# Token rows on SP's queue, the overflow loop moved from the end to expert pair 10, and a new order of scatter and turning in a one-core mixer + MoE kernel

## The chip, the cores and the metric

One core of a Trainium2 chip runs the whole kernel. The metric is device time in microseconds (us) of one execution. The engines are TensorE (PE, with PEld for its weight loads), VectorE (DVE), ScalarE (ACT), GpSimd (POOL) and SyncE (SP, which only issues DMAs here); a "q" behind a name is that engine's sequencer or DMA queue. All arithmetic is float32, with float32 split in two where the program calls for more exactness.

## The reference, cut to what matters

512 tokens of width 1024, one layer. A hybrid mixer of four branches comes first; then a two-level mixture of experts, which the change touches: 4 groups of 8 experts, each token takes the best group and in it the best two experts.

```python
x = x + g1 * hybrid_mixer(rms_norm(x) * (1 + sc1) + sh1, ...)
h = rms_norm(x) * (1 + sc2) + sh2
g_p, g_idx = top_k(softmax(h @ wg + bg), 1)
top_v, top_i = top_k(expert logits of that group, 2)
gate = g_p * softmax(top_v)
for each expert e, on its tokens xe:                 # 32 experts, D = 1024, inner width 512
    y = (silu(xe @ w1[e]) * (xe @ w3[e])) @ w2[e]
    x += g2 * (gate * y summed back onto the tokens)
```

## The kernel before

**Mixer and routing.** Up to about 790 us the mixer runs; its weights come on SP's queue. The last output projection (`w_out`) and the router's logits are computed in two halves of 256 tokens. `route(half)` (L1132) finds groups, experts, gates and ranks of a half on DVE; for each of its two 128-token tiles ACT writes the normalised rows into the one buffer `xg[0]` (L1145) and stores them to the DRAM table `xhd` (L1147, ACT's queue in before). Route of half 1 runs under a hand-written order of DVE; `meanwhile()` (L1111) puts a few matmuls without a user (`scr`) on PE between the two steps of that route, as many as `WARM` says. `toki` holds, for each pair of experts, the 128 token numbers (64 for each expert); `fetch(p)` (L1122) gathers these rows from `xhd` into `xg[p % 2]`, on POOL's queue.

**Expert stream.** The experts are taken two at a time, as 16 pairs p. A pair's weights are 12 tiles of 1 MB in the order of use: 8 for `front` (w1, w3), 4 for `product` (w2); pair 15 has 18, most of them smaller, so that there are 198 loads in all. They land in a ring of 20 SBUF slots. `stream()` (L1089) hands tile i out and calls `load_to(i + 20)` (L1080), so the load of tile i + 20 is issued on SP (L1086) as soon as its slot is free. The compiled program counts these loads on eight counters in turn (DMAHW0 to DMAHW7): load n goes out when load n-8 has landed.

**Loop over pairs** (L1489 on), PE's order written out by hand: `product(p-1)` (two groups of matmuls into `py`), `parts(p-1)` (DVE and ACT split `py` into `yh` and `yl`), `front(p)` (64 matmuls into `ph`), then `add` of pair p-1: for each half of the columns and each of 4 token tiles t two matmuls into `po` (PE) that scatter the rows back by the 0/1 matrix `pT`, and one DVE addition into `xm` (L1408). Among the adds stand `turn_in(p+1)` (L1327: eight PE transposes of `xg` into `xT`, eight evacuations into `xe`, odd ones on DVE and even ones on ACT, then `fetch(p+2)`) and `turn` (L1370: four transposes of `g`, evacuated into `gT`).

**Overflow.** 64 slots for each expert hold the usual load. Tokens past that are handled by `overflow()` (L1413): a loop on the chip (`For_i`, L1418) whose count `n_ob` is read at run time from `eobi`. In before it stands behind pair 15's front and adds and ahead of pair 15's four products. With these inputs the count is zero: the trace has not one `ov` weight load of the loop's body.

Of the kernel before, what the change touches and what calls it, by code (L numbers as in the profile page):

```python
# [9 lines left out]
F32 = mybir.dt.float32  # L10
F32R = mybir.dt.float32r
# [11 lines left out]
KD = D // 128  # L23
NT = S // 128
# [5 lines left out]
RL = (10, 11, 18, 19)  # L30
WS = (10, 3, 6, 6, 12)
LATE = 4
WARM = (1, 2, 2, 2, 4)
LNEXP = "natural_log_exp_and_others"


# [1 line left out]
def trunk(ctx, tc, x, c, ada_w, ada_b, norm1_g, norm2_g, w_in, hgrn_lb, hgrn_norm_g, conv_w, conv_b, conv_ln_g,  # L38
          conv_ln_b, sb_qnorm_g, sb_knorm_g, ret_norm_g, w_branch, w_gate, b_gate, w_out, router_group_w,
          router_group_b, router_expert_w, router_expert_b, expert_w1, expert_w3, expert_w2, out):  # L40
    nc = tc.nc
# [169 lines left out]
    for t in range(NT):  # L211
        A.activation(sq0, xt[t], AF.Square, accum_out=ssq[:, t:t + 1])
    pe_order = ctx.enter_context(ExitStack())
# [3 lines left out]
        engines={mybir.EngineType.DVE, mybir.EngineType.Activation}))  # L217
# [814 lines left out]
    xhd = dram.tile([S, D], F32, name="xhd")  # L1032
# [17 lines left out]
    ewx = ctx.enter_context(tc.tile_pool(name="ewx", bufs=EWX, side="right"))  # L1050
# [24 lines left out]
    ring = [(ewx, "ew")] * EWX + [(wst, tag) for tag in ("raw", "raw", "wh", "wh", "wl", "wl")]  # L1075
# [4 lines left out]
    def load_to(n):  # L1080
        while len(loaded) < min(n, len(order)):
            pool, tag = ring[len(loaded) % len(ring)]
            w = pool.tile([128, 2048], F32, name="ew", tag=tag)
            src = order[len(loaded)]
            w = w[:, :src.shape[1] * src.shape[2]].rearrange("p (k c) -> p k c", k=src.shape[1])
            nc.sync.dma_start(w, src)  # L1086
            loaded.append(w)
# [34 lines left out]
    def fetch(p):  # L1122

        P.indirect_dma_start(out=xg[p % 2], out_offset=None, in_=xhd[:, :],  # L1124
                             in_offset=bass.IndirectOffsetOnAxis(ap=toki[:, p:p + 1], axis=0),
                             bounds_check=S - 1, oob_is_err=False)
# [5 lines left out]
    def route(half, pl, between=None):  # L1132
# [10 lines left out]
        for i in range(2):  # L1143
            xs = xg[0]
            A.activation(xs, xm[:, 2 * half + i], AF.Copy, scale=r[:, i:i + 1])  # L1145
            t = 2 * half + i
            nc.scalar.dma_start(xhd[t * 128:(t + 1) * 128], xs)  # L1147
        gm, gi, og = first_max(lg[:, :, :4], 4, "f0")
        then(og[:, 1])
        ge = nr.tile([128, 2, 4], F32, name="ge", bufs=2)  # L1150
# [19 lines left out]
        for i in range(2):  # L1170
            t = 2 * half + i
# [77 lines left out]
    pe_order = ctx.enter_context(ExitStack())  # L1249
    for half in range(2):  # L1250
        pl = ps_o.tile([128, 512], F32, name="pl", tag="o1")
        ts = slice(2 * half, 2 * half + 2)
        cbs = (0, 1, 2, 3) if half == 0 else (2, 3, 0, 1)
        for n, cb in enumerate(cbs):
            if half == 0 or cb < 2:
                wo[cb] = wblock(w_out, 0, KD, cb * 256, 256)
            w = wo[cb]
            if half and n == 3:
                load_to(EWX)
            cs = slice(cb * 256, cb * 256 + 256)  # L1260
            o = psm()
            for i in range(2):
                three(o[:, i * 256:(i + 1) * 256],
                      tuple((lambda k, a=a: a[:, k, i * 128:(i + 1) * 128]) for a in (mh[half], ml[half])),
                      tuple((lambda k, a=a: a[:, k, :]) for a in w), KD, first=i == 0)
            y = yo[n % 2]
            V.tensor_mul(y, o.rearrange("p (t c) -> p t c", t=2), g1b[:, None, cs].to_broadcast([128, 2, 256]))
            (V if half else P).tensor_add(xm[:, ts, cs], xm[:, ts, cs], y)
            for i in range(2):
                A.activation(y[:, i], xm[:, 2 * half + i, cs], AF.Square,  # L1270
                             accum_out=sq2[:, 2 * half + i, cb:cb + 1])
            if n:
                logits(half, pl, n - 1, cbs[n - 1])
        between = None
        if half:
            pe_order.enter_context(tc.manual_schedule(engines={mybir.EngineType.PE}))
            between = meanwhile()
        logits(half, pl, 3, cbs[3], between)
        if half:
            next(between)  # L1280
        if half:
            with tc.manual_schedule(engines={mybir.EngineType.DVE}):
                route(half, pl, between.send)
        else:
            route(half, pl)

# [38 lines left out]
    ew = stream()  # L1325

    def turn_in(p):  # L1327

        pt = psz("xT").rearrange("p a (b c) -> p (a b) c", c=128)
        xe = moe.tile([128, KD, 128], F32, name="xe", bufs=1)  # L1330
        for d in range(KD):
            a, k = divmod(d, 4)
            T.transpose(pt[:, d], xg[p % 2][:, a * 512 + k:(a + 1) * 512:4], ident)  # L1333
        for d in range(KD):
            if d % 2:
                V.tensor_scalar(xe[:, d], pt[:, d], a2s[:, d:d + 1], sh2s[:, d:d + 1], op0=OP.mult, op1=OP.add)
            else:
                A.activation(xe[:, d], pt[:, d], AF.Identity, scale=a2s[:, d:d + 1], bias=sh2s[:, d:d + 1])
        if p < 14:
            fetch(p + 2)  # L1340
        return xe

    def front(p, xe):

# [14 lines left out]
    class Back:  # L1359
# [10 lines left out]
        def turn(self):  # L1370
            pg = ps_o.tile([128, 512], F32, name="gTp", tag="o1")
            for f in range(4):
                T.transpose(pg[:, f * 128:(f + 1) * 128], self.g[:, f::4], ident)
            self.gT = moe.tile([128, 512], F32, name="gT", tag="yh") if self.p < 15 else ewx.tile([128, 512], F32, name="gT", tag="ew")
            A.activation(self.gT, pg, AF.Copy)

        def product(self, n):
# [35 lines left out]
    def overflow():  # L1413
# [2 lines left out]
        base = keep.tile([128, 1], F32, name="base")  # L1416
        V.memset(base, 0.0)
        with tc.For_i(0, n_ob) as i:  # L1418
            e = nc.sync.value_load(eobi[0:1, bass.ds(i, 1)], min_val=0, max_val=31)

            def wload(src, kk, c0):
                w = moe.tile([128, 512], F32, name="ov", tag="yl")
                r0 = kk // 4 * 512
                nc.sync.dma_start(w, src[0][bass.ds(e, 1), r0:r0 + 512, c0:c0 + 512].rearrange(
                    "o (p k) c -> p k (o c)", k=4)[:, kk % 4])
                return w

            sk = keep.tile([128, 2, NT], F32, name="s4", bufs=2)
            V.tensor_scalar(sk, oslot, base, None, op0=OP.subtract)
            pr_ = moe.tile([128, NT, 128], F16, name="pr_", tag="pT", bufs=1)  # L1430
            e0_ = moe.tile([128, 512], F32, name="e0_", tag="yh")
            gt_ = moe.tile([128, NT, 128], F32, name="gt_", tag="yh")
            for t in range(NT):
                V.tensor_scalar(e0_[:, :128], io[:, :128], sk[:, 0, t:t + 1], None, op0=OP.is_equal)
                V.scalar_tensor_tensor(pr_[:, t], io[:, :128], sk[:, 1, t:t + 1], e0_[:, :128], op0=OP.is_equal,
# [12 lines left out]
            V.tensor_scalar(toki[:, 0:1], pg_[:, 2:3], 1024.0, None, op0=OP.add)  # L1448
            fetch(0)
            V.tensor_scalar(go[:, 1:2], pg_[:, 2:3], 1024.0, None, op0=OP.add)  # L1450
            pT = ewx.tile([128, 512], F32R, name="ovpT", tag="ew")
            V.tensor_scalar(pT, io, go[:, 1:2], None, op0=OP.is_equal)
            xo = moe.tile([128, KD, 128], F32, name="xe", bufs=1)
            ps = psz("ovx")
# [5 lines left out]
            for j, src in enumerate((expert_w1, expert_w3)):  # L1460
                for kk in range(KD):
                    mm(ph[:, j], xo[:, kk], wload(src, kk, 0), kk == 0, kk == KD - 1)
            g = moe.tile([128, 512], F32, name="g", tag="yh")
            A.activation(g, ph[:, 0], AF.Sigmoid)
            V.tensor_mul(g, g, ph[:, 0])
            V.scalar_tensor_tensor(g, g, go[:, 0:1], ph[:, 1], op0=OP.mult, op1=OP.mult)
            pg = psm("ovT")
            for f in range(4):
                T.transpose(pg[:, f * 128:(f + 1) * 128], g[:, f::4], ident)
            gT = moe.tile([128, 512], F32, name="gT", tag="yh")  # L1470
            A.activation(gT, pg, AF.Copy)
            for hf in range(2):
                cs = slice(hf * 512, hf * 512 + 512)
                py = psm("ovy")
                for kk in range(4):
                    mm(py, gT[:, kk * 128:(kk + 1) * 128], wload(expert_w2, kk, hf * 512), kk == 0, kk == 3)
                V.tensor_mul(py, py, g2b[:, cs])
                yh = moe.tile([128, 512], F32R, name="yh", tag="yh")
                yl = moe.tile([128, 512], F32R, name="yl", tag="yl")
                split(yh, yl, py)  # L1480
                for t in range(NT):
                    po = psm("ovo")
                    mm(po, pT[:, t * 128:(t + 1) * 128], yh, True, False)
                    mm(po, pT[:, t * 128:(t + 1) * 128], yl, False, True)
                    V.tensor_add(xm[:, t, cs], xm[:, t, cs], po)
            V.tensor_scalar(base, base, 128.0, None, op0=OP.add)


    b, nxt = None, turn_in(0)  # L1489
    for p in range(16):  # L1490
        if b:
            for n in range(2):
                b.product(n)
            for n in range(2):
                b.parts(n)
            b.places()
        xe = nxt
        g = front(p, xe)
        if p == 1:
            eobi, oslot = overflow_tables()  # L1500
        late_, b = b, Back(p, g)
        if late_:
            late_.add(0, (0, 1, 2))
        if p < 15:
            nxt = turn_in(p + 1)
        if late_:
            late_.add(0, (3,))
            late_.add(1, (0,))
        b.turn()
        if late_:  # L1510
            late_.add(1, (1, 2, 3))
    pe_order.close()
    overflow()
    pe_order.enter_context(tc.manual_schedule(engines={mybir.EngineType.PE}))
    b.places()
    for n in range(4):
        b.product(n)
# [27 lines left out]
```

## Time and profile before

| | us |
|---|---|
| median of 3 runs | 1298.15 (1297.8 to 1303.95) |
| the profiled execution, its own time | 1301.55 |
| span of that execution, first to last instruction | 1299.8 |
| PE busy in the span | 1230.8 (95%) |
| DVE busy | 692.3 (53%) |
| ACT busy | 467.0 (36%) |
| POOL busy | 210.7 (16%) |

The expert stream fills the stretch from about 827 to 1275 us. The mean shares hide that PE and the DMA engines are both near their limit there, so rows are read by stretch, and idle time is read with the wait that ended it: `[4.74 <-SPq L1418]` behind a row means that the engine stood 4.74 us before it and that an event of SP's sequencer at line 1418 released it.

### The profile page before, as it was taken

To read this page: it belongs to the slowest core of one execution; us is meant where nothing else is said; L and a number is where in the kernel's file an instruction comes from. 1 tells how busy PE (TensorE), PEld (TensorE's weight loads), DVE (VectorE), ACT (ScalarE), POOL (GpSimd) and SP (SyncE) were. 2 spreads that over 40 slices of the span, in tenths; PEclk is the share of its full clock that TensorE was granted. 3 is DMA by queue.
4 is the path that set the end of the run, shared out by engine and by line. 5 is a ranking of instruction groups with operands and counts; after the bars stand their busy time and mean duration, and the time that the engine had idled before them with its cause. 6 is when DMAs were issued, how large, how long until landed. Compare 5 with 4: busy or idle time off the path is not lost. (4 is left out here: it accounts for less than half of the span.)

```text
span 1299.8 us, 17074 instructions
## 1 busy us (share of the span) xinstructions
PE 1230.8 (95%) x6818; PEld 855.0 (66%) x6818; DVE 692.3 (53%) x1105; ACT 467.0 (36%) x665; POOL 210.7 (16%) x171
## 2 busy tenths in 40 slices
PE   7999988999999999998999999799999999999997
PEld 5789888987779987787888897333333433333344
DVE  2724679998963564457865435235333443433334
ACT  3447565446544455453335533111111111111110
POOL 3226746201110111212211110100000000000000
PEclk8999997999999999999999999899999999999998
DMA  9332311132222322226775298699999999999994
GB/s 337 130 120 66 97 40 59 33 97 66 77 86 66 98 65 73 89 90 211 234 232 185 92 386 342 246 416 419 420 418 419 420 419 419 419 419 419 420 403 161
DMA packets 108477, 299.23 MB, mean 230 GB/s; under 512 B 9704, under 2 KB 65112, under 8 KB 84588
## 3 DMA queue, kind: packets, MB, share of 16 engines
q1 hardware_dynamic: 102312, 289.45, 58.5%
q10 hardware_dynamic: 3300, 4.36, 1.0%
q0 software_dynamic: 2784, 4.31, 1.0%
q8 instruction: 54, 0.88, 0.3%
q14 instruction: 27, 0.22, 0.0%
HBM read 298.08 MB, written 4.20 MB: 233 GB/s over the span
## 5 line engine op out<-in xcount | busy, mean ns | idle before, releaser
L58 PE MATMUL ph<-ew,xe 128*64 128x512 f32 x1024 | 229.8, 597 | 7.2 <-DMA ew<-in_expert_w_dram 6.6
L58 PEld LDWEIGHTS ph<-ew,xe 128*64 128x64 f32 x1024 | 77.4, 138 | 156.6 <-issue 135.3
L58 PE MATMUL mm<-hh,wh 128*128 128x512 f32 x448 | 178.8, 399 | 0.0
L254 DVE TENSOR_TENSOR wl<-raw,wh 128x2048 fp32r<-128x2048 f32 x55 | 131.8, 2396 | 85.6 <-ACT wh L253 83.9
L58 PE MATMUL mm<-hh,wl 128*128 128x512 f32 x448 | 174.9, 390 | 1.6 <-DVE wl L266 1.6
L58 PE MATMUL mm<-hl,wh 128*128 128x512 f32 x448 | 174.8, 390 | 0.0
L1408 DVE TENSOR_TENSOR xm<-xm,po 128x512 f32<-128x512 f32 (+1 forms) x136 | 85.8, 648 | 153.5 <-PE po L58 153.3
L253 ACT ACTIVATE wh<-raw 128x2048 fp32r<-128x2048 f32 x55 | 105.2, 1912 | 70.4 <-PE mm L58 70.0
L58 PE MATMUL mm<-wh,hh 128*128 128x256 f32 x448 | 130.4, 291 | 0.0
L58 PE MATMUL mm<-wl,hh 128*128 128x256 f32 x448 | 127.4, 284 | 0.0
L58 PE MATMUL mm<-wh,hl 128*128 128x256 f32 x448 | 127.4, 284 | 0.0
L58 PE MATMUL py<-ew,gT 128*64 128x512 f32 (+1 forms) x544 | 117.6, 586 | 5.4 <-SPq L1418 4.7
L58 PEld LDWEIGHTS mm<-hh,wh 128*128 128x128 f32 x448 | 84.2, 188 | 23.5 <-issue 7.2
L58 PEld LDWEIGHTS mm<-hh,wl 128*128 128x128 f32 x448 | 84.1, 188 | 19.7 <-DVE wl L266 1.9
L58 PEld LDWEIGHTS mm<-hl,wh 128*128 128x128 f32 x448 | 84.2, 188 | 16.5 <-DVE hl L206 0.3
L58 PEld LDWEIGHTS mm<-wh,hh 128*128 128x128 f32 x448 | 86.5, 193 | 6.0 <-issue 5.8
L58 PEld LDWEIGHTS py<-ew,gT 128*64 128x64 f32 x544 | 38.8, 142 | 75.7 <-issue 72.7
L58 PEld LDWEIGHTS mm<-wl,hh 128*128 128x128 f32 x448 | 86.6, 193 | 0.2
L58 PEld LDWEIGHTS mm<-wh,hl 128*128 128x128 f32 x448 | 86.5, 193 | 0.0
L1124 POOL DMA_INDIRECT xg<-xhd,toki x16 | 16.0, 1000 | 394.6 <-PE xT L1333 346.5
L157 ACT ACTIVATE yh<-py 128x512 fp32r<-128x512 f32 (+1 forms) x34 | 19.5, 572 | 160.1 <-DVE py L1396 160.1
L1354 ACT ACTIVATE g<-ph 128x512 f32<-128x512 f32 x16 | 9.6, 598 | 176.3 <-PE ph L58 176.3
(435 smaller groups left out, 2055.8 us busy)
## 6 DMA issues: line engine op xcount, KB each, us to landing
ew<-in_expert_w_dram SPq DMA_DIRECT2D x186, 1024.0 KB, 19.9
raw<-in_w_in_dram SPq DMA_DIRECT2D x26, 1024.0 KB, 4.9
raw<-in_w_gate_dram SPq DMA_DIRECT2D x16, 1024.0 KB, 5.6
adaw<-in_ada_w_dram SPq DMA_DIRECT2D x64, 256.0 KB, 3.4
aw<-in_ada_w_dram SPq DMA_DIRECT2D x32, 256.0 KB, 5.4
raw<-in_w_branch_dram SPq DMA_DIRECT2D x8, 1024.0 KB, 5.7
raw<-in_w_out_dram SPq DMA_DIRECT2D x6, 1024.0 KB, 6.0
ew<-in_expert_w_dram SPq DMA_DIRECT2D x12, 512.0 KB, 12.9
```

Of the source, the lines that this page charges most:

```text
L58: T.matmul(o, l, r, start=start, stop=stop, skip_group_check=True)
L157: A.activation(h_ap, src, AF.Copy)
L253: a = A.activation(wh, raw, AF.Copy)
L254: v = V.tensor_sub(wl, raw, wh.bitcast(F32))
L1124: P.indirect_dma_start(out=xg[p % 2], out_offset=None, in_=xhd[:, :], in_offset=bass.IndirectOffsetOnAxis(ap=toki[:, p:p + 1], axis=0), bo ...
L1354: A.activation(g, ph[:, 0], AF.Sigmoid)
L1408: V.tensor_add(xm[:, t, cs], xm[:, t, cs], po)
```

## The change

1. `WARM[3]` goes from 2 to 0: two of the matmuls without a user go.
2. The four stores of token rows to `xhd` move from ACT's queue to SP's (L1147), and SP joins DVE in the hand-written order around route of half 1, with `load_to(len(ring))` inside it. So the first weight loads are issued on SP among and behind the stores.
3. `turn_in` becomes a generator in two steps: transposes and `fetch(p+2)`; later the evacuations into `xe`, now all on ACT (for pair 0 still on both).
4. The loop over pairs places all four `add(0)` ahead of the transposes of `turn_in`, and the evacuations behind `turn`.
5. `overflow()` moves behind pair 10's front and adds (`OVP = 10`). For pair 11 the transposes, `fetch(12)` and the evacuations stand behind it. The loop's reads and weight loads go to POOL's queue, and its tiles take other buffers; the `gT` of pair 15 uses the common buffer `yh`.

```diff
-WARM = (1, 2, 2, 2, 4)
+WARM = (1, 2, 2, 0, 4)
+OVP = 10
...
-            nc.scalar.dma_start(xhd[t * 128:(t + 1) * 128], xs)
+            nc.sync.dma_start(xhd[t * 128:(t + 1) * 128], xs)
...
-            with tc.manual_schedule(engines={mybir.EngineType.DVE}):
+            with tc.manual_schedule(engines={mybir.EngineType.DVE, mybir.EngineType.SP}):
                 route(half, pl, between.send)
+                load_to(len(ring))
...
     def turn_in(p):
...
             T.transpose(pt[:, d], xg[p % 2][:, a * 512 + k:(a + 1) * 512:4], ident)
+        if p < 14 and p != OVP:
+            fetch(p + 2)
+        yield
+        xe = moe.tile([128, KD, 128], F32, name="xe", bufs=1)
         for d in range(KD):
-            if d % 2:
+            if d % 2 and not p:
                 V.tensor_scalar(xe[:, d], pt[:, d], ...)
             else:
                 A.activation(xe[:, d], pt[:, d], AF.Identity, ...)
-        if p < 14:
-            fetch(p + 2)
-        return xe
+        yield xe
...
-            self.gT = moe.tile([128, 512], F32, name="gT", tag="yh") if self.p < 15 else ewx.tile([128, 512], F32, name="gT", tag="ew")
+            self.gT = moe.tile([128, 512], F32, name="gT", tag="yh")
...
-            e = nc.sync.value_load(eobi[0:1, bass.ds(i, 1)], min_val=0, max_val=31)
+            e = nc.gpsimd.value_load(eobi[0:1, bass.ds(i, 1)], min_val=0, max_val=31)
...
-        xe = nxt
         g = front(p, xe)
         if p == 1:
             eobi, oslot = overflow_tables()
+        nxt = turn_in(p + 1) if p < 15 else iter(())
         late_, b = b, Back(p, g)
         if late_:
-            late_.add(0, (0, 1, 2))
-        if p < 15:
-            nxt = turn_in(p + 1)
+            late_.add(0)
+        if p != OVP:
+            next(nxt, None)
         if late_:
-            late_.add(0, (3,))
             late_.add(1, (0,))
         b.turn()
+        if p != OVP:
+            xe = next(nxt, None)
         if late_:
             late_.add(1, (1, 2, 3))
-    pe_order.close()
-    overflow()
-    pe_order.enter_context(tc.manual_schedule(engines={mybir.EngineType.PE}))
+        if p == OVP:
+            pe_order.close()
+            overflow()
+            fetch(p + 2)
+            pe_order.enter_context(tc.manual_schedule(engines={mybir.EngineType.PE}))
+            next(nxt)
+            xe = next(nxt)
```

In the rows of the order, `L1086` of before is `L1087` of after, `L1147` is `L1148` and `L1418` is `L1421`; `xN` counts like instructions in a row. SP's queue around the first expert loads, before:

```order
L250 DMA raw<-in_w_out_dram 128x8x256 x4
L1086 DMA ew<-in_expert_w_dram 128x2048 x2
L250 DMA raw<-in_w_out_dram 128x8x256
L1086 DMA ew<-in_expert_w_dram 128x2048
L250 DMA raw<-in_w_out_dram 128x8x256
L1086 DMA ew<-in_expert_w_dram 128x2048 x183
```

The same place after, down to the loop's count (TENSOR_LOAD):

```order
L251 DMA raw<-in_w_out_dram 128x8x256
L1087 DMA ew<-in_expert_w_dram 128x2048 x3
L1148 DMA xhd<-xg_5967 128x1024
L1087 DMA ew<-in_expert_w_dram 128x2048
L1148 DMA xhd<-xg_5967 128x1024
L1087 DMA ew<-in_expert_w_dram 128x2048 x3
L1148 DMA xhd<-xg_5967 128x1024 x2
L1087 DMA ew<-in_expert_w_dram 128x2048 x137
L1418 TENSOR_LOAD eobi
```

The four stores now stand among the first loads, with ten loads of the ring's first filling behind the last store, and 147 loads are queued ahead of the loop's count, 51 behind it. PE's adds and transposes in one pair of the steady loop, before:

```order
L58 MATMUL po<-yl,pT 128x512
L1333 MATMUL xT<-ident,xg_5967 128x128 x8
L58 MATMUL po<-yh,pT 128x512
L58 MATMUL po<-yl,pT 128x512
L58 MATMUL po<-yh,pT 128x512
L58 MATMUL po<-yl,pT 128x512
L1373 MATMUL gTp<-ident,g 128x128 x4
```

And after:

```order
L59 MATMUL po<-yl,pT 128x512
L1334 MATMUL xT<-ident,xg_5967 128x128 x8
L59 MATMUL po<-yh,pT 128x512
L59 MATMUL po<-yl,pT 128x512
L1376 MATMUL gTp<-ident,g 128x128 x4
```

One add moved from behind the transposes `xT` to ahead of them. PE at the end of the loop `For_i`, with the semaphores that the rows wait for (the list is cut by the view), before:

```order
L1418 UNCONDITIONAL_BRANCH [waits DMASW5_49,DMASW4_49,DMASW6_49,DMASW3_49,DMASW7_49,DMASW2_49,DMAHW0_49,DMASW1_49,DMAHW1_49,DMASW0_49,DMAHW2_49,SP_sequencer_49,DMAHW3_49,DVE_sequencer_49,DMAHW4_49,PE_sequencer_49,DMAHW5_49,Activation_s
L58 MATMUL py<-ew,gT 64x256 x16
```

And after:

```order
L1421 UNCONDITIONAL_BRANCH [waits DMASW5_49,DMASW4_49,DMASW6_49,DMASW3_49,DMASW7_49,DMASW2_49,DMAHW0_49,DMASW1_49,DMAHW1_49,DMASW0_49,DMAHW2_49,SP_sequencer_49,DMAHW3_49,DVE_sequencer_49,DMAHW4_49,PE_sequencer_49,DMAHW5_49,Activation_s
L1334 MATMUL xT<-ident,xg_6828 128x128 x8
L59 MATMUL py<-ew,gT 64x512 x16
```

The same wait, which names all DMA counters and the other engines, stood ahead of pair 15's products and now stands ahead of pair 11's transposes and pair 10's products.

## Rows read from the trace of the kernel before

**Rows 1.** Windows: busy us of each engine (instructions), granted clock, DMA share, GB/s.

```profile
core 0: us, PE busy (x) PEld busy (x) DVE busy (x) ACT busy (x) POOL busy (x), PEclk, DMA share, GB/s
791.00:807.00 16.00, 15.25 (x118) 13.63 (x118) 4.87 (x15) 4.74 (x14) 0.00 (x0) 1.00 0.74 275
818.00:833.00 15.00, 8.50 (x52) 3.89 (x53) 3.96 (x18) 3.11 (x5) 4.08 (x4) 0.66 0.27 87
833.00:1140.00 307.00, 296.16 (x1367) 119.79 (x1364) 118.49 (x260) 45.23 (x88) 10.91 (x11) 0.99 1.01 417
1140.00:1270.00 130.00, 120.12 (x530) 50.06 (x529) 42.84 (x76) 16.79 (x33) 1.98 (x2) 1.00 1.01 413
1280.00:1284.00 4.00, 3.82 (x18) 2.19 (x20) 0.58 (x2) 0.00 (x0) 0.00 (x0) 0.50 0.01 2
```

**Rows 2.** Timeline of PE, pairs 4 to 11: start, length, work, [idle before, releaser].

```profile
959.87 7.09 PE L58 MATMUL py<-ew,gT 128*64 128x512 f32 x32
985.49 0.50 PE L58 MATMUL po<-yh,pT 128*128 128x512 f32 x1 [0.18 <-DVE xm L1408]
986.87 0.50 PE L58 MATMUL po<-yh,pT 128*128 128x512 f32 x1 [0.64 <-DVE xm L1408]
987.53 7.09 PE L58 MATMUL py<-ew,gT 128*64 128x512 f32 x32
...
1120.46 1.11 PE L1333 MATMUL xT<-ident,xg 128*128 128x128 f32 x8
...
1125.87 7.09 PE L58 MATMUL py<-ew,gT 128*64 128x512 f32 x32
1132.79 7.89 PE L58 MATMUL ph<-ew,xe 128*64 128x512 f32 x34
1140.94 3.65 PE L58 MATMUL ph<-ew,xe 128*64 128x512 f32 x16 [0.26 <-DMA ew<-in_expert_w_dram]
```

**Rows 3.** Timeline of PE around the overflow loop at the end.

```profile
1275.04 0.40 PE L58 MATMUL po<-yl,pT 128*128 128x512 f32 x1
1280.18 5.72 PE L58 MATMUL py<-ew,gT 128*64 128x256 f32 x32 [4.74 <-SPq L1418]
...
1287.28 1.95 PE L58 MATMUL py<-ew,gT 128*64 128x256 f32 x16
```

**Rows 4.** Line 1418, the loop: sequencer events of SP and PE, who waited for it.

```profile
L1418 SPq EVENT_SEMAPHORE  x21: 17/28/28, 1273.6 to 1280.8; - x21
...
L1418 PEldq EVENT_SEMAPHORE  x13: 51/51/51, 1276.6 to 1279.8; - x13
...
L1418 PEldq COMPARE_BRANCH  x3: 97/187/310, 1276.5 to 1279.9; - x3
...
  PE py L58: 4.7, 1
  DVE pT L1368: 3.7, 1
```

**Rows 5.** Timeline of SP's queue: expert loads and their issue times.

```profile
801.62 2.54 SPq L1086 DMA_DIRECT2D ew<-in_expert_w_dram  x5
832.35 4.24 SPq L1086 DMA_DIRECT2D ew<-in_expert_w_dram  x4
...
1143.45 0.33 SPq L1086 DMA_DIRECT2D ew<-in_expert_w_dram  x1
...
1164.66 0.33 SPq L1086 DMA_DIRECT2D ew<-in_expert_w_dram  x1
...
1267.77 4.51 SPq L1086 DMA_DIRECT2D ew<-in_expert_w_dram  x3
```

**Rows 6.** DMA issues from 740 us, to 1144 and to 1165: count, KB, us to landing.

```profile
ew<-in_expert_w_dram SPq DMA_DIRECT2D x147, 1024.0 KB, 19.9
xg<-xhd,toki POOLq DMA_INDIRECT x14, 8.1
...
ew<-in_expert_w_dram SPq DMA_DIRECT2D x155, 1024.0 KB, 20.0
```

**Rows 7.** Waits of SP's queue, 836 to 1145 us: total, times, longest.

```profile
SPq L1086 <- DMA ew<-in_expert_w_dram: 179.5, 86, 3.7
```

**Rows 8.** Timeline of ACT and POOL: row stores of half 1, first gather.

```profile
807.34 0.33 ACTq L1147 DMA_DIRECT2D xhd<-xg  x1
...
816.09 1.15 ACT L1145 ACTIVATE xg<-xm,rr 128x1024 f32<-128x1024 f32 x1 [8.12 <-DMA xhd<-xg]
817.27 0.33 ACTq L1147 DMA_DIRECT2D xhd<-xg  x1
...
820.76 1.09 POOL L1124 DMA_INDIRECT xg<-xhd,toki  x1 [47.78 <-DVE ga L1220]
```

**Rows 9.** Timeline of PE at the start of pair 0.

```profile
810.03 1.98 PE L58 MATMUL scr<-xm,ident 128*128 128x512 f32 x4
...
824.45 1.95 PE L1333 MATMUL xT<-ident,xg 128*128 128x128 f32 x8 [4.41 <-DMA xg<-xhd,toki]
827.00 15.62 PE L58 MATMUL ph<-ew,xe 128*64 128x512 f32 x64 [0.60 <-ACT xe L1338]
```

## What the change will do to the time, predicted before it ran

> **What bounds the kernel now.** I read the windows by stage first, since the shares of the whole span mix stages with different limits [rows 1]. From 833 to 1140 us PE is busy 296.16 of 307 us and the DMA engines are full at 417 GB/s; from 1140 to 1270 the DMA share is still 1.01, but PE drops to 120.12 of 130. The timeline of PE says which of the two ends last [rows 2]: up to pair 11 a pair takes PE 27.67 us (959.87 to 987.53) and its only waits are 0.18 and 0.64 us for DVE's additions; in pair 11's front the first wait for a weight tile appears (1140.94, 0.26 us), and from there the stream of weights sets the pace. So ahead of 1130 the loads fall behind PE without hurting it, because the ring of 20 tiles was full; by 1140 that lead is used up. Then the end [rows 3, 4]: PE finishes pair 15's adds at 1275.4, stands 4.74 us at the overflow loop although the loop has no turn to make, and starts the last four products at 1280.18.
>
> What the loop waits for is the point of this case. SP issues its last load at 1272.3 (1267.77 + 4.51) [rows 5] and then spends 1273.6 to 1280.8 in 21 semaphore events of the loop's line; PE and DVE are let go together, DVE after 3.7 us, PE after 4.7 [rows 4]. The order names the wait: all DMA counters and all engines, on every engine, also when no turn is made. So the loop is a drain: nobody passes before every load issued ahead of it has landed. At the end that costs little, since the stream is over anyway.
>
> **The change, part by part.**
>
> *The loop at pair 10.* Ahead of it SP's queue now holds 147 loads, that is up to tile 146, while pair 10's front uses tiles up to 127: the ring's whole lead of 19 tiles must land. PE comes to this place at 1125.87 (in before pair 10's products start there) [rows 2]. In before load 147 goes out at 1143.45, the 147th of the expert loads up to then [rows 5, 6]; with 19.9 us to landing it is there at 1163.4. The other bound is 1164.66, where load 155, the next on the same counter, goes out [rows 5, 6]; SP's long wait in this stretch is for exactly such landings (179.5 us in 86 waits) [rows 7]. I take 1164.7. So PE stands some 39 us. It is no stall that other work covers: DVE, ACT and POOL wait at the same place, and the eight transposes for pair 11 and `fetch(12)` now stand behind it.
>
> *Shift of the stream by the first loads.* In before all 20 loads of the first filling are out by 804.2 (801.62 + 2.54), and SP then has no free slot until 832.35 [rows 5]; from 818 to 833 the DMA engines work at 0.27 [rows 1]. In after ten of the 20 stand behind the last row store. The first store of half 1 goes out at 807.3 as now; its landing is bounded by 3.5 us (817.27 to the gather at 820.76, nothing beside it) and 8.7 us (807.34 to 816.09, five loads beside it) [rows 8]. With ten loads held back the transfer is nearly alone, so 3.5: 810.8, then ACT's 1.15 us of the second tile, second store at 812, loads behind it. Ten loads at 2.51 us (1.05 MB at 417 GB/s) end at 837.4, where in before load 21 starts at 832.35: the stream is 5 us later. With 8.7 us it is 10 later; a gain isn't in sight, but should the stores come out sooner than I think it may be 0. Bounds 0 to +10.
>
> The Trainium skill, page "Perfetto Trace Analysis", section "DMA Optimizations", speaks against this part: above all with loops or control flow it may make sense to give inputs to one DMA-issuing engine and outputs to another. The rows of before show both sides of it: with loads in flight beside it the store took 5 us more, while the loads on their own queue stood behind nothing. Going by the rule the loads should have kept SP's queue to themselves and the shift would be 0, 5 us less in the sum; going by the store's rows alone the move would be a gain. The sum takes the loss, since the loads and not the stores set the end of the drain.
>
> *`WARM`, the earlier gather, ACT freed of its waits for stores.* Two matmuls of 0.99 us go (half of the 1.98 us at 810.03) [rows 9], and ACT no longer holds the route's small steps for 8.12 us [rows 8]. PE's start of pair 0 may come some 2 us before 827.00 (in before 4.41 us idle for the gather, evacuation 0.60) [rows 9]. I cost all of this at nothing: what PE gains ahead of pair 10 it waits out at the drain, whose end is set by the loads. The same goes for the new order of adds and evacuations in pairs 0 to 9.
>
> *Behind the drain.* First the end of the loop: 13 events of 51 ns and three branches of 187 ns on PE's sequencer, 1.2 us, of which part lies ahead of the wait [rows 4]; 1.0. Then eight transposes. PE has stood for 40 us, and in before the granted clock after the 4.74 us stop is 0.50, the lower level of 1.2 GHz [rows 1]; eight such transposes after 4.41 us of idling took 1.95 us [rows 9], against 1.11 in the steady loop [rows 2]. I take 1.95 (bounds 1.1 and 1.95). The first products pay too: the 32 of 5.72 us after the stop would be 3.9 at twice the 1.95 us of the next 16 [rows 3], a loss of 1.8. Bounds 0 and 1.8.
>
> From product 10 to product 15 it is five pairs. All 19 tiles of lead are in SBUF, so PE sets the pace: 27.67 less the two waits of 0.82 for DVE [rows 2], which no longer has four evacuations between the adds, is 26.85; upper bound 27.67, if these waits stay. One of the five has no transposes (pair 15; pair 11's are counted above), 0.9 less. So 5 x 26.85 - 0.9 = 133.4, upper bound 138.3. The weights don't hold PE up: 51 loads, 45 tiles' worth of 1.05 MB, at 413 GB/s are 114 us, less than 133 [rows 1]. The tail from product 15 takes 19.6 (1280.18 to 1299.8) [rows 3]; without the stop ahead of it, 1.8 less: 17.8. For the same reason the 4.74 us go.
>
> **Sum.** 1164.7 + 5 + 1.0 + 1.95 + 1.8 + 133.4 + 17.8 = 1325.7 for the span, against 1299.8: 26 us more. The profiled execution takes 1.75 us more than its span, 1327.4; it stood 3.4 above the median of the runs (1301.55 against 1298.15), so 1324. As a difference: 39 us of standing and 5 of shift are put in; the weight waits of pairs 11 to 15 (about 3 us a pair: 30.6 against 27.67), the DVE waits, the stop and slow products at the end are got back. All low bounds: 1163.4 + 0 + 1.0 + 1.1 + 0 + 133.4 + 17.8 = 1316.7, as a time 1315. All high: 1164.7 + 10 + 1.2 + 1.95 + 1.8 + 138.3 + 17.8 = 1335.7, as a time 1334.
>
> **Rivals.**
>
> *The wait doesn't reach the lead of the ring (not slower).* If the end of the loop covered only loads that PE or SP has already taken notice of, or if only SP waited, PE would pass at 1126 and the stream of weights would go on setting the end. Then 4.74 us and 1.8 us of slow products go, and up to 5 us of shift come: 1299.8 - 6.5 + 5 = 1298.3, as a time about 1297. For it: the loop makes no turn. Against it: SP's 21 events and the 4.7 us of PE at the same line now [rows 4]. The point from which it decides: the sum comes to 1299.8 if the drain ended at 1164.7 + 5 - 25.9 = 1143.8, that is nine or ten loads earlier than tile 146. Chance 0.07.
>
> *The early part gains and the drain is cheap (faster).* The same with a stream that starts 5 us or more earlier instead of later: below 1292. Against it stand ten loads behind the stores. Chance 0.02.
>
> *The stream starves PE behind the drain.* SP's queue stands too; after it only the slots that PE frees can be filled, and if the gathers or the restart of loads cost it more than the 19 us of slack (133 - 114), pairs 14 and 15 wait for weights and the end moves to 1336 to 1345. Against it: 417 and 413 GB/s in all stretches [rows 1]. Chance 0.04.
>
> **How the numbers follow.** The drain with its full lead has the remaining 0.87. Its range is 1315 to 1334 by the bounds; I make it 1312 to 1335 for the scatter of runs, and the other cases outside it hold 0.13. About 0.5% (6.5 us) is what a measurement of this kernel tells from no change: below 1291.7 is faster, 0.02; 1291.7 to 1304.6 the same, 0.07; above, slower, 0.91.
>
> **What would show it.** In the profile of after PE has one idle of 40 to 50 us between pair 10's last add and the transposes of pair 11, released from the loop's line; all other engines have it as well; the DMA share falls to near nothing for a few us before its end; pairs 11 to 15 run at 26.9 to 27.7 us with no weight waits; the last stop of 4.74 us is gone; load 21 goes out some 5 us later. Wrong I would be if PE's idle there were under 15 us, or if pairs 11 to 15 still waited for weights.

## The result, and the profile after

| | before | after |
|---|---|---|
| median, us | 1299.64 (1297.8 to 1303.95) | 1320.49 (1318.15 to 1323.93) |
| profiled execution: time / span, us | 1301.55 / 1299.8 | 1321.34 / 1319.2 |
| ratio, 95% interval | 1 | 1.0158 [1.0122, 1.0194] |

The change makes the kernel 1.6% slower, 20.9 us; 1324 was predicted as the time. The stop of TensorE is there, where the sum needed it, and a little shorter: 40.47 us, where the terms of the sum make it some 45. The chain that ended last (start, us, what), which in before can be followed back only to the last products, now leads through the stop:

```profile
1123.45 21.42 DMA ew<-in_expert_w_dram
...
1144.93 19.86 DMA ew<-in_expert_w_dram
1164.79 1.12 issue
1165.91 1.98 PE xT L1334 x8
1167.89 8.10 PE py L59 x32
1175.98 13.73 PE ph L59 x64
```

Read it from below: the products of pair 10 (`py`) wait for the transposes of pair 11, these for the exit of the loop (1.12 us), and this for load 147, which went out at 1144.93 and was 19.86 us under way. That load carries tile 146 (tiles count from 0), which PE needs only in pair 12. "issue" is time in which the engine waited for nothing that the profile shows. The waits by engine and line (us in total, times, longest) tell the same of PE and of SP:

```profile
PE xT L1334 <- issue: 40.5, 1, 40.5
PE ph L59 <- DMA ew<-in_expert_w_dram: 8.4, 8, 1.3
...
SPq L1421 <- DMA ew<-in_expert_w_dram: 17.4, 2, 15.0
```

One wait of 40.5 us stands on PE. The profile names no releaser for it; SP, in the loop's line, waits for expert weights. The 8.4 us that `ph` waits for weights lie ahead of the loop, in pairs 7 to 10. PE's timeline around the stop, to be held beside [rows 2]:

```profile
1024.42 3.65 PE L59 MATMUL ph<-ew,xe 128*64 128x512 f32 x14 [0.72 <-DMA ew<-in_expert_w_dram]
...
1095.43 7.09 PE L59 MATMUL py<-ew,gT 128*64 128x512 f32 x32
...
1125.04 0.40 PE L59 MATMUL po<-yl,pT 128*128 128x512 f32 x1
1165.91 1.98 PE L1334 MATMUL xT<-ident,xg 128*128 128x128 f32 x8 [40.47 <-issue]
1167.82 8.17 PE L59 MATMUL py<-ew,gT 128*64 128x512 f32 x32
...
1195.47 7.09 PE L59 MATMUL py<-ew,gT 128*64 128x512 f32 x32
...
1222.05 7.09 PE L59 MATMUL py<-ew,gT 128*64 128x512 f32 x32
...
1301.76 3.67 PE L59 MATMUL py<-ew,gT 128*64 128x256 f32 x32
```

PE is done with pair 10's adds at 1125.4, as in before, although up to pair 6 its pairs are 1.1 us shorter (26.58 us): from 1024 on it has caught up with the stream, and a pair takes 28 to 31 us. In before the first such wait came at 1140.94 [rows 2]. Behind the stop a pair takes 26.58 us (1195.47 to 1222.05) against 27.67 in [rows 2] and about 30.6 in before's pairs 11 to 14, with no wait for weights, and the last products follow at 1301.76 without the 4.74 us of [rows 3]. The windows show what the DMA engines do meanwhile:

```profile
core 0: us, PE busy (x) PEld busy (x) DVE busy (x) ACT busy (x) POOL busy (x), PEclk, DMA share, GB/s
1125.50:1157.00 31.50, 0.00 (x0) 0.00 (x0) 0.93 (x2) 0.00 (x0) 0.00 (x0) 0.56 1.01 417
1157.00:1161.00 4.00, 0.00 (x0) 0.00 (x0) 0.00 (x0) 0.00 (x0) 0.00 (x0) 0.50 0.88 367
1161.00:1165.50 4.50, 0.00 (x0) 0.00 (x0) 0.00 (x0) 0.00 (x0) 0.00 (x0) 0.50 0.18 75
1166.00:1170.00 4.00, 4.00 (x14) 2.25 (x16) 0.28 (x1) 2.07 (x7) 1.98 (x2) 0.50 0.80 265
1170.00:1290.00 120.00, 120.00 (x562) 48.36 (x560) 40.00 (x64) 22.73 (x53) 1.98 (x2) 1.00 0.98 394
```

For 31.5 us every engine stands and the loads run on at 417 GB/s; then for 4.5 us the DMA engines stand as well (0.18); then PE, at the lower clock level (0.50, 1.2 GHz) for its first 4 us, is busy in 120 of 120 us. Behind the loop the bound has moved from the stream to PE, which has stood for 40 us.

At the start of the stream, SP and ACT against [rows 5] and [rows 8]:

```profile
803.82 4.18 SPq L1148 DMA_DIRECT2D xhd<-xg  x2
808.09 71.91 SPq L1087 DMA_DIRECT2D ew<-in_expert_w_dram  x33
```

```profile
802.64 1.15 ACT L1146 ACTIVATE xg<-xm,rr 128x1024 f32<-128x1024 f32 x1 [0.82 <-DVE rr L149]
...
806.50 1.15 ACT L1146 ACTIVATE xg<-xm,rr 128x1024 f32<-128x1024 f32 x1 [2.05 <-DMA xhd<-xg]
```

Ahead of the second row tile ACT stands 2.05 us for the first store instead of 8.12, and the ten loads go out from 808.1, where in before all were out by 804.2.

### The profile page after: what moved, and what is told of

Its sections match the earlier page's. It is cut to its first block, busy times and chain, and to the rows that moved or that the text cites. A ratio compares the mean times of both kernels' runs of the same rounds, so it can differ in the third digit from the quotient of the medians.

```text
span 1319.2 us, 17065 instructions
## 1 busy us (share of the span) xinstructions
PE 1224.5 (93%) x6814; PEld 854.1 (65%) x6814; DVE 672.3 (51%) x1045; ACT 482.9 (37%) x725; POOL 210.8 (16%) x172
## 4 chain that ended last, share of the span: by engine, by line
PE 68%; DMA 19%; DVE 5%; ACT 4%; POOL 2%; issue 2%; SPq 0%; POOLq 0%; ACTq 0%; DVEq 0%
PE mm L59 40%; DMA ew<-in_expert_w_dram 16%; PE ph L59 11%; PE py L59 5%; PE po L59 3%; DMA aw<-in_ada_w_dram 2%; PE z L59 2%; PE sbe L59 1%; PE xT L1334 1%; ACT wh L254 1%; POOL sf L578 1%; PE sbz L59 1%; PE sbo L59 1%; POOL hgf L579 1%; DVE wl L255 1%
## 5 line engine op out<-in xcount | busy, mean ns | idle before, releaser
L1411 DVE TENSOR_TENSOR xm<-xm,po 128x512 f32<-128x512 f32 (+1 forms) x136 | 81.7, 648 | 155.5 <-PE po L59 155.2
L1343 ACT ACTIVATE xe<-xT,mod 128x128 f32<-128x128 f32 x124 | 47.2, 473 | 91.0 <-PE xT L1334 89.5
```

## The experiments

Executions end the mixer up to 8 us apart: the first scaling of a row tile (`xg`, half 0) starts between 768.3 and 776.5 us in the profiles below. Where spans are compared they are therefore also counted from that row (775.61 in before, 773.55 in after); "from the row" means that; such a comparison is of one execution of each. Times are medians beside runs of the kernel before on the same chip. Of before's later medians 1298.18 belongs to loop_end, only_loop10, lead8 and loop_pair3, 1297.69 to stores_act, no_loop, loop_split and split_15, and 1296.73 to lead14 and loop_first.

| kernel | median, us | ratio to before, 95% | PE's stop at the loop, us | end of span from the row |
|---|---|---|---|---|
| before | 1299.64, later 1298.18, 1297.69, 1296.73 | 1 | 4.74 | 524.2 |
| after | 1320.49 | 1.0158 [1.0122, 1.0194] | 40.47 | 545.7 |
| loop_end | 1303.84 | 1.0049 [1.0035, 1.0062] | 4.73 | 528.9 |
| only_loop10 | 1316.65 | 1.0137 [1.0112, 1.0162] | 38.86 | 546.1 |
| lead14 | 1311.17 (one run) | | 27.79 | 534.5 |
| lead8 | 1303.32 | 1.0038 [1.0022, 1.0054] | 12.56 | 527.3 |
| loop_pair3 | 1305.51 | 1.0053 [1.0037, 1.0069] | 23.05 | 529.9 |
| stores_act | 1298.51 | 1.0004 [0.9991, 1.0017] | 4.67 | 524.3 |
| no_loop | 1295.48 | 0.9976 [0.9961, 0.9990] | none | 522.0 |
| loop_split | 1306.03 | 1.0049 [1.0031, 1.0067] | 3.45 | 529.6 |
| split_15 | 1305.62 | 1.0051 [1.0034, 1.0067] | 3.48 | 529.0 |
| loop_first | 1291.13 | 0.9953 [0.9936, 0.9970] | 6.00 (with the gather) | 518.2 |

**loop_end: the loop undone, the rest kept.**

```diff
-        if p == OVP:
-            pe_order.close()
-            overflow()
...
+    pe_order.close()
+    overflow()
+    pe_order.enter_context(tc.manual_schedule(engines={mybir.EngineType.PE}))
     b.places()
```

> The changed kernel with its overflow loop back behind pair 15's adds; everything else of the change stays. Theory (the loop drains the ring's lead of 19 tiles, that is the whole loss): PE's stop of 40.5 us at pair 10 goes, the stop of about 5 us at the end comes back, load 147 goes out some 1.5 us later than before (1144.93 against 1143.45), so the time is 1299 to 1304. Rival (the row stores on SP's queue or the new order of adds cost as well): 1308 or more.

1303.84 us: the stop of 40 us is gone and with it 15 of the 21 us that were lost (20.9 less 5.7). What stays, 0.49% of before, is clear of its interval and at the upper end of what was expected; it is taken up in stores_act.

**only_loop10: the loop's move alone (with its queue, its buffers and pair 11's transposes behind it), everything else as in before.**

```diff
-    pe_order.close()
-    overflow()
-    pe_order.enter_context(tc.manual_schedule(engines={mybir.EngineType.PE}))
+        if p == OVP:
+            pe_order.close()
+            overflow()
+            fetch(p + 2)
+            pe_order.enter_context(tc.manual_schedule(engines={mybir.EngineType.PE}))
+            nxt = turn_in(p + 1)
```

> The kernel before with only the loop moved to pair 10 (its queue and buffers as in the change, pair 11's turning behind it); row stores, the matmuls without a user, the order of adds and evacuations as before. Theory: PE stops about 38 us at pair 10, passes at 1164 to 1166, and then runs five pairs at the old 27.67 us instead of 26.58, so the time is 1321 to 1327, a little above the changed kernel. Rival (the loop alone costs little and another part of the change makes the loss): 1305 or less.

The ratio is 1.0137, which the interval of after's 1.0158 covers: the loop's move by itself is the loss. The stop is 38.86 us and the pairs behind it take 27.67 us, both as expected; PE passes at 1161.96, 2 us ahead of the expected 1164:

```profile
1161.96 1.98 PE L1334 MATMUL xT<-ident,xg 128*128 128x128 f32 x8 [38.86 <-issue]
1163.87 8.50 PE L59 MATMUL py<-ew,gT 128*64 128x512 f32 x32
...
1192.94 7.09 PE L59 MATMUL py<-ew,gT 128*64 128x512 f32 x32
...
1220.61 7.09 PE L59 MATMUL py<-ew,gT 128*64 128x512 f32 x32
```

The median of 1316.65 missed the expected 1321 to 1327; the profiled execution, 1321.87, lies in it, but it is the slowest of the four. From the row both kernels end alike (546.1 and 545.7): here the stream of loads is not held back at the start, there the pairs behind the stop are 1.1 us shorter each, and the two nearly cancel.

**lead8 and lead14: the same loop at pair 10 with fewer loads ahead of it.** `128 + 8` or `128 + 14` caps what is loaded before the loop.

```diff
-            load_to(i + len(ring))
+            load_to(min(i + len(ring), 136) if i < 128 else i + len(ring))
```

> The changed kernel, loop at pair 10, but ahead of the loop only tiles up to 135 are loaded (a lead of 8 tiles instead of 19); the other 11 loads are issued behind the loop. Theory (the stop lasts until the last load issued ahead has landed): PE's stop shrinks from 40.5 to about 12.6 us, as load 136 lands 11 x 2.51 us earlier; the DMA engines idle some 8 us around the loop, which the stream of weights carries to the end: 1300 to 1307. Rival (a loop in the middle of the program has a fixed price): the stop stays near 40 us and the time near 1320.

> The changed kernel with tiles up to 141 loaded ahead of the loop at pair 10, a lead of 14. Theory (2.51 us of stop for each load of lead): PE's stop is 12.6 + 6 x 2.51 = 27.6 us. Rival: anything off that line by more than 2 us.

PE's row behind the loop, first lead8, then lead14:

```profile
1137.95 1.98 PE L1334 MATMUL xT<-ident,xg 128*128 128x128 f32 x8 [12.56 <-DMA ew<-in_expert_w_dram]
```

```profile
1154.60 1.98 PE L1334 MATMUL xT<-ident,xg 128*128 128x128 f32 x8 [27.79 <-DMA ew<-in_expert_w_dram]
```

12.56, 27.79 and 40.47 us with 8, 14 and 19 tiles of lead: 2.54 us a tile in both steps ((27.79 - 12.56) / 6 and (40.47 - 27.79) / 5), about the 2.51 us that a tile takes to load. When PE arrives, 3 to 4 tiles of the lead are down in each of the three; in after (1164.79 - 1125.44) / 2.51 = 15.7 of the 19 are still to land. So the stop is the loads in flight and queued, and the exit of the loop of about 1 us; with a lead of 8 the kernel with a loop at pair 10 is back at 1303.32. In both the profile itself names expert loads as the releaser.

**loop_pair3: the same loop with the full lead, seven pairs earlier** (`OVP = 3`).

> The changed kernel with the loop at pair 3 instead of 10, with the full lead ahead of it. Theory: PE stops 22 to 28 us there (it comes at 925, load 63 lands at about 950), but 12 pairs are left, in which PE works through tiles that are already there while the loads are the bound again by the end; what remains is the 8 to 10 us in which the DMA engines stand: 1301 to 1308. Rival (a stop of PE is lost wherever it lies): 25 us more than a kernel without it, 1316 or more.

PE stops 23.05 us, yet the kernel ends as loop_end does (1305.51 and 1303.84, intervals that overlap). A stop of PE early in the stream is no loss of its own: behind it PE uses tiles that are there already and meets the stream again at the end. What is lost is what the DMA engines lose:

```profile
935.00:947.00 12.00, 0.00 (x0) 0.00 (x0) 0.00 (x0) 0.00 (x0) 0.00 (x0) 0.50 0.82 339
947.00:955.00 8.00, 7.20 (x28) 3.33 (x30) 0.49 (x1) 2.90 (x8) 0.99 (x1) 0.69 0.47 166
955.00:1270.00 315.00, 306.82 (x1412) 126.54 (x1408) 105.14 (x169) 58.16 (x134) 8.90 (x9) 1.00 1.01 418
```

0.18 of 12 us and 0.53 of 8 us are 6.4 us of standing DMA engines, and from the row the last load lands 7.0 us later than in loop_end (516.2 against 509.2). The stop at the end that it saves is worth about as much: 4.73 us and 1.5 of slow products. At pair 10 the same standing costs nothing, as PE is the bound behind it; there PE's stop counts. One price or the other is paid, by which of the two is the bound until the end.

**stores_act: loop at the end, and the stores, first loads and `WARM` as in before**, so that only the order of adds and evacuations is new.

```diff
-            nc.sync.dma_start(xhd[t * 128:(t + 1) * 128], xs)
+            nc.scalar.dma_start(xhd[t * 128:(t + 1) * 128], xs)
...
-            with tc.manual_schedule(engines={mybir.EngineType.DVE, mybir.EngineType.SP}):
+            with tc.manual_schedule(engines={mybir.EngineType.DVE}):
                 route(half, pl, between.send)
-                load_to(len(ring))
```

> The changed kernel with the loop at the end, and also the row stores back on ACT's queue, the first loads and the two matmuls without a user as in the kernel before; so only the order of adds, transposes and evacuations is new. Theory (with the loop at the end the stream of weights sets the end, and the 0.4% that this kernel with the changed stores lost came from the ten first loads held back): load 147 goes out as in before, no loss: 1296 to 1300, level with before. Rival (the new order of adds costs): 1302 or more.

1.0004: level. So the new order of adds, although it takes 1.1 us off a pair, is worth nothing while the stream sets the end. The 0.4 to 0.5% of loop_end is the price of the stores ahead of the first loads: from the row the last load lands 5.6 us later in loop_end (509.2 against 503.6) and the kernel ends 4.6 us later (528.9 against 524.3); the two medians, 1303.84 and 1298.51, are 5.3 us apart. This agrees with what the Trainium skill, page "Perfetto Trace Analysis", section "DMA Optimizations", says on giving inputs and outputs different issuing engines. `WARM` went back in the same run and has not been tried by itself; that the weights land later speaks for the stores and loads.

**no_loop: without the loop** (tokens past 64 of an expert would be left out; these inputs have none).

```diff
-    pe_order.close()
-    overflow()
-    pe_order.enter_context(tc.manual_schedule(engines={mybir.EngineType.PE}))
     b.places()
```

> The changed kernel without the overflow loop (the part that computes tokens past 64 of an expert is left out; these inputs have none). Theory: against the kernel with the loop at the end only the stop of 4.7 us and the slow products behind it (1.5 to 1.9 us) go, 5 to 7 us less: 1296 to 1299. Rival (the weights still in flight hold the last products anyway): 1301 or more.

1295.48, just under the expected range: 8.4 us less than loop_end by the medians, 6.9 from the row, where 5 to 7 were expected. PE goes from the last add straight into the last products:

```profile
1278.64 3.67 PE L59 MATMUL py<-ew,gT 128*64 128x256 f32 x32
```

So the weights that these products need first had landed by then: the whole 4.7 us at the end are the loop's, as are the slow products behind them (5.16 us in loop_end). That makes 6.2 us; where the rest comes from stays open.

**loop_split: the loop between the third and the last product of pair 15**, the stores of the first three column blocks behind it.

```diff
     for n in range(4):
+        if n == 3:
+            b.add(2)
+            pe_order.close()
+            overflow()
+            pe_order.enter_context(tc.manual_schedule(engines={mybir.EngineType.PE}))
+            b.places()
+            for m in range(3):
+                b.store(m)
         b.product(n)
```

> The changed kernel with the loop between the third and the last product of pair 15, the stores of the first three column blocks behind it. Theory: the weights have landed by the time PE comes there, so the drain has nothing left to wait for; only its own steps remain (1 to 3 us) instead of 4.7 and the slow products: 1298 to 1302. Rival (the loop's price is its fixed steps, not the loads): as with the loop ahead of all four products, 1303 or more.

My theory missed here and the rival was right: 1.0049, as with the loop ahead of the products. The DMA engines had been idle for some 7 us (nothing moved behind 1285), and still PE stops:

```profile
1291.43 0.28 PE L59 MATMUL po<-yl,pT 128*128 128x256 f32 x1
1295.16 3.68 PE L59 MATMUL py<-ew,gT 128*64 128x256 f32 x16 [3.45 <-issue]
```

What PE's sequencer does meanwhile stands in the rows of the loop's lines: ten semaphore events, then the read of the count (0.49 us), then this, with three branches:

```profile
L1426 PEldq EVENT_SEMAPHORE  x13: 51/51/51, 1293.1 to 1294.8; - x13
```

So there is a fixed price beside the drain: 3.45 us in which the engines read the count, meet and branch, and 1.7 us of slow product behind it (3.68 against 1.95). Where enough loads are in flight it hides behind them, as at pair 10. At the end both are there: the chain of loop_end still leads through the landing of the last load,

```profile
1273.12 8.56 DMA ew<-in_expert_w_dram
1281.68 0.85 issue
1282.53 5.16 PE py L59 x32
```

but of before's 4.74 us only about 1.3 (4.74 - 3.45) hang on it; most would remain without. The stores that were moved behind the loop don't explain the time: from the last add to the end of the span it takes 3.9 us here and 4.0 in loop_end.

**split_15: as loop_split, with five of the ten held back loads ahead of the last two row stores** (`load_to(15)` ahead of `route`).

> As with the loop between the third and the last product, and five of the ten held back loads (up to the 15th) go out ahead of the two row stores of half 1. Theory: these five fill the time from 785 to 800 us in which the DMA engines stood at 0.10, the other five are done before PE frees the first slot, so the stream starts 2 to 4 us earlier: 1294 to 1298. Rival (the hold at the start costs nothing): level with the kernel without the five.

Level with loop_split, so no gain. But this run doesn't test the hold alone: the last row store goes out 12.3 us behind the one before it, the gather comes late, and pair 0 starts at 833.40, 56.9 from the row, against 50.9.

```profile
806.63 12.63 SPq L1148 DMA_DIRECT2D xhd<-xg  x2
819.35 29.76 SPq L1087 DMA_DIRECT2D ew<-in_expert_w_dram  x13
```

```profile
812.00:820.00 8.00, 6.12 (x58) 2.73 (x57) 1.94 (x13) 1.24 (x2) 0.00 (x0) 0.82 0.03 13
```

In the 8 us ahead of 820 the DMA engines stand at 0.03, since SP waits for the last row tile with the next loads behind it: one queue for stores that wait and loads that needn't. The row tile is late because on ACT it now stands behind a small step of the route, for which ACT waits for DVE; in after it came ahead of that step:

```profile
817.66 0.20 ACT L1201 ACTIVATE dv<-dv 128x2 f32<-128x2 f32 x1 [10.40 <-DVE dv L1200]
817.77 1.13 ACT L1146 ACTIVATE xg<-xm,rr 128x1024 f32<-128x1024 f32 x1
```

What the five loads gained early was lost there: from the row load 64 goes out only 0.9 us earlier than in loop_split (157.5 against 158.4). So whether the hold itself costs is read from stores_act and not from this run.

**loop_first: a version that beats both kernels.** From stores_act; the loop stands right behind the routing, ahead of pair 0, and only its count is computed ahead of it.

```diff
+    n_i, nb0, ends = overflow_tables()
+    pe_order.close()
+    overflow()
+    fetch(1)
+    pe_order.enter_context(tc.manual_schedule(engines={mybir.EngineType.PE}))
     b, xe = None, list(turn_in(0))[1]
...
         with tc.For_i(0, n_ob) as i:
+            eobi, oslot = block_tables(nb0, ends)
```

> The order of adds of the change, row stores on ACT's queue as before, and the overflow loop right behind the routing, ahead of pair 0, with only its count computed ahead of it (the block tables inside the loop). Theory (the loop costs its fixed steps of some 3.5 us plus the landing of what is in flight): there the first 20 loads are nearly all landed and PE waits for the first gather anyway, so pair 0 starts only 2 to 4 us later, while the stop of 4.7 us and the slow products at the end go: 1293 to 1297, 1 to 5 us less than before. Rival (the fixed steps lie in full on the way to pair 0, and the stream carries them to the end): level with before, 1297 to 1300.

0.9953 [0.9936, 0.9970]: 5.6 us less than before; against the change's 1.0158 it is some 2% less. Up to rounding the order of additions into `xm` doesn't matter, so the loop can stand anywhere behind the routing; here 19 of the 20 loads of the ring's first filling are out ahead of it (the last at 797.1, the 20th behind the loop at 820.0), the DMA share from 812 to 820 us is 0.27, and PE waits for the first gather anyway. Pair 0 starts 1.7 us later from the row (53.1 against 51.4), and at the end nothing stops:

```profile
820.31 1.98 PE L1338 MATMUL xT<-ident,xg 128*128 128x128 f32 x8 [6.00 <-issue]
822.84 14.98 PE L59 MATMUL ph<-ew,xe 128*64 128x512 f32 x64 [0.55 <-ACT xe L1347]
```

```profile
1270.20 3.67 PE L59 MATMUL py<-ew,gT 128*64 128x256 f32 x32
```

Against stores_act, which has the same stores and order of adds, it ends 6.1 us earlier from the row (518.2 against 524.3): the stop of 4.67 us and 2.1 of slow products go, and the later start takes a little of it back. It gains more than no_loop (0.9976), whose row stores are still on SP's queue, and leaves nothing out.

## Why the prediction was right, step by step

- **The bound and the drain.** Right: the loop holds every engine until the last load issued ahead of it has landed, although it makes no turn (chain of after; 2.54 us a tile of lead in lead8, lead14 and after).
- **Landing of load 147.** Predicted 1169.7 (1164.7 and 5 of shift), measured 1164.79. The lower of the two bounds was right: it was 19.86 us under way, so 1163.4 in before; 1.3 of the miss. The shift came out at 1.5 us instead of 5. Of this 2.1 is scatter (the mixer of this execution was earlier by so much); from the row load 147 goes out 3.5 us later (371.4 against 367.8). The stream as a whole is later by about what was predicted: from the row load 21 lands 5.8 us later (67.8 against 61.9), load 136 5.1 (363.8 against 358.7). So 5 was a fair price; but the sign that the prediction gave for it, that load 21 goes out some 5 us later, did not come: it goes out at the same time from the row (56.7) and lands later, as the ten held back loads are ahead of it. One step of the working was wrong as well: "The first store of half 1 goes out at 807.3 as now". It went at 803.8; 2.1 us of that is the same scatter, and why it is 1.5 us earlier from the row (30.3 against 31.7) no run shows.
- **Exit of the loop.** 1.0 predicted, 1.12 measured behind a drain. But the reading of the stop at the end was half right: the landing of the last load does end it (chain of loop_end), yet without any load in flight 3.45 of the 4.74 us would remain (loop_split).
- **Transposes and products at the lower clock.** 1.95 and 1.8 predicted; from 1165.91 to 1167.82 it is 1.91, and the products lose 1.1 (8.17 against 7.09).
- **Pairs behind the drain.** 133.4 predicted without that loss; 1167.82 to 1301.76 less 1.1 is 132.9. A pair takes 26.58, not 26.85: besides DVE's waits a little more went. That the weights don't hold PE up was right: PE is busy in 120 of 120 us from 1170 to 1290.
- **Tail.** 17.8 predicted, 17.4 measured.
- **Sum.** 1325.7 for the span, 1319.2 measured; 4.9 of the 6.5 us are the landing. As a time 1324 against 1320.49 is closer than the span mostly by scatter: 3.4 us were taken off because before's profiled execution stood so much above its median, while after's stood 0.9 above its own.
- **Edits priced at nothing.** Right for the end, as far as the runs show: the order of adds is worth nothing while the stream is the bound (stores_act). But what PE gains ahead of pair 10 is not waited out at the drain, as the prediction has it: PE had already waited it out for weight tiles in pairs 7 to 10 (8.4 us). That it came to the loop at 1125.4, as the sum had taken from before, is therefore in part luck; the sum didn't need it, since the loads end the stop. `WARM` alone wasn't tried.
- **Rivals.** That the wait wouldn't reach the ring's lead fell with the chain; an earlier stream fell with load 136, which lands 5.1 us later from the row; starving pairs behind the drain were not seen. PE's stop is put down to "issue" and not to the loop's line, as the prediction had it; that it is the loads is shown by the chain and by lead8 and lead14, where the profile names them.

## What to carry to other kernels

In this kernel a loop with a run-time count is a barrier on all engines and on all DMAs issued ahead of it, even when it makes no turn. So it belongs where little is in flight and PE waits anyway, not where a prefetch ring is full. PE's stop there lasts until the last load issued ahead has landed (here 2.5 us for each load still to land) and about 1 us more, and at least as long as the fixed steps (3.45 us). Whether such a stop of PE, or the standing of the DMA engines, costs the kernel time is decided by which of the two is the bound from there to the end: 23 us of stop at pair 3 cost next to nothing against the loop at the end (1305.51 and 1303.84), 40 us at pair 10 cost some 15. Stores that wait for an engine should not stand in the queue of a prefetch: what the store gains in quiet, the loads behind it lose (5.3 us here).

## What the runs showed that I had not expected

- The end of a drain is ragged: in the last 4.5 us the DMA share is 0.18 at 75 GB/s, after 1.01 up to 1157. On average 3 of the 16 engines (0.18 x 16) are still at work, and the loop waits for the last.
- The shorter pairs didn't bring PE to the loop any earlier: from pair 7 on it waited for the stream, four pairs sooner than in before.
- The loop's fixed steps cost PE 3.45 us with nothing in flight, and another 1.7 in the products that follow at the lower clock level (granted clock 0.50 from 1295.2 to 1299 in loop_split).
- Executions that are alike up to there (before, only_loop10, stores_act, loop_first) differ by up to 7 us already at the end of the mixer (768.3 to 775.6), which is more than most of the effects here; spans compare better from a common row.
